# Modulation of the second layer: three sixths row chunk by row chunk on TensorE in the first MLP, the last sixth in the second MLP

## The chip, the cores and the metric

The kernel runs on one core of one Trainium2 chip. The metric is the device time of one execution, in microseconds (us). One execution was also profiled; its trace gives the start and the length of every instruction on the engines: TensorE (PE, its weight loads are PEld), VectorE (DVE), ScalarE (ACT), GpSimd (POOL) and SyncE, whose queue SP issues nearly all transfers.

## What is computed

Two layers over 512 latent tokens (`x`) and 256 context tokens (`c`), 1024 wide, in float32. Each layer modulates its normalised tokens by shift, scale and gate vectors that come from a conditioning vector, one for each of the two token kinds; this modulation is what the change touches:

```python
for l in range(DEPTH):
    last = l == DEPTH - 1
    mod_x = (jax.nn.silu(c) @ w_ada[l] + b_ada[l])[:, None, :]
    sh1, sc1, g1, sh2, sc2, g2 = jnp.split(mod_x, 6, axis=-1)
    mod_c = jax.nn.silu(c_ctx) @ w_ada[l] + b_ada[l]
    csh1, csc1, cg1, csh2, csc2, cg2 = jnp.split(mod_c, 6, axis=-1)
    ...
    hx = rmsnorm(x, g_pre_mix[l]) * (1.0 + sc1) + sh1
    ...
    x = x + g1 * rmsnorm(y, g_post_mix[l])
    hx2 = rmsnorm(x, g_pre_ff[l]) * (1.0 + sc2) + sh2
    x = x + g2 * rmsnorm(squared_relu_mlp(hx2, w_ff1[l], w_ff2[l]), g_post_ff[l])
```

`w_ada[l]` is 1024 x 6144, so each sixth (shift, scale, gate for the mixing, then the same for the MLP) is a product of a vector with a 1024 x 1024 matrix. In the last layer only shift and scale of the mixing (`csh1`, `csc1`) are still needed for the context tokens. The MLP is `square(relu(h @ w1)) @ w2` with 4096 hidden features.

## The kernel before

**Precision.** Large products run in float32r: each operand is split into a high and a low part, and a product takes three matmuls (high by high, high by low, low by high). Splitting a weight costs a cast on ScalarE (`hi`, or the first half of a tile `Wf`) and a subtraction on VectorE or GpSimd (`lo`, the second half). All raw weights, those of the modulation too, go through the same four buffers (tag "raw", 512 KB each); a load is issued by SP, in program order of its queue, as soon as the buffer it takes has been released.

**The MLP of a layer** runs in 16 hidden groups of 256 features (groups 0 to 15). Groups 0 and 1 are plain (`ff1`, tiles `h...`). For groups 2 to 15 the first product of the latent tokens is done in Winograd's form: `wino_open` builds seven weight operands from two raw tiles (casts L1147, low parts L1148, differences L1152), `wino` multiplies them (L1182, tiles `w` and `wt`; those with `t` take sums `S` of token blocks, made by `wino_a`, L952 to L956) and multiplies the context tokens plainly (L1195, `wc`); `hidden` squares the result (L1122 to L1125), and L1201 adds partial sums. The second product (`ff2`, tiles `f2`, layer, group, token kind, L1247) then goes token block by token block, six blocks in layer 0 and four in layer 1, and VectorE adds its PSUM result to `Y` (L1251).

**The modulation** is a generator, `ada_quad`, one per sixth `(l, q)`. It loads `w_ada` in eight row chunks of 128 rows (tile `wa`, L252) and has two ways to use them:

- With `side` (an accumulator in SBUF): VectorE multiplies a chunk by its 128 entries and adds it up, `acc` (L264 the first, L266 the others), one instruction per chunk and token kind, each followed by a `yield`. After the last chunk TensorE sums over the 128 partitions with a stationary operand that has a column of ones (L272): four matmuls per token kind, each 32 columns of the array wide.
- Without `side`: TensorE multiplies each chunk (L279), four matmuls per chunk, both token kinds at once (they are two of the 32 columns of `silu`); they accumulate in one PSUM tile over the eight chunks. One `yield` per chunk.

Both end in the same way: the row is copied to SBUF (`arow`) and turned into columns, or, for a gate (q = 2 or 5), multiplied by its gain and written to DRAM.

After each block of `ff2` from group 1 on, the MLP loop takes one step of the generator (`next(ada, None)`), and behind the last group it takes what is left. In layer 0 that is the gate of its own MLP, `(0, 5)`, and all six sixths of layer 1; all seven go with `side`: `(0, 5)`, `(1, 0)` and `(1, 1)` for two token kinds (16 steps each), the other four for one (8 each), 80 in all. Earlier sixths of layer 0 go without `side` beside the attention.

The program's order is not the engines' order: a scheduler reorders instructions within each engine by priority and by when it thinks that their operands are there; each engine then runs its list in order.

Of the kernel before, what the change touches and what calls it, by code (L numbers as in the profile page):

```python
# [3 lines left out]

# [14 lines left out]
P = 128  # L19
# [12 lines left out]
# How far the first product of the MLP goes ahead of other work.  # L32
HP = 5
# The engine (v or p) that takes each of the two-operand steps of a hidden group: low parts of the weights of the
# first and second product, differences of weights, low parts of the hidden features.
# [10 lines left out]
# What the tensor engine does beside the attention units of a layer: U, G, F load the weights of a column group  # L46
# of the in-projection and u, g, f project a token block with them, fc, fx step through the Fourier mixing,
# gc, gx load the gates, oc, ox step through the output projection, ada through a modulation.
# [13 lines left out]
def _bc(ap, n, axis):  # L62
    """ap with a broadcast dimension of n put in at free position `axis`."""
    v = ap.unsqueeze(axis)
    shape = list(v.shape)
    shape[axis] = n
    return v.to_broadcast(shape)
# [3 lines left out]
def kernel(ctx: ExitStack, tc: tile.TileContext, a: dict, out: bass.AP):  # L71
# [15 lines left out]
    # Temporaries of a chain come from h1, h2, h3 in this order, so that chains never wait in a circle.  # L87
# [9 lines left out]
    # Streams that run side by side have tiles of their own; within a tag tiles are handed out in program order.  # L97
# [25 lines left out]
    F = bank("F", 3)  # L123
# [9 lines left out]
    # ------------------------------------------------------------- constants  # L133
# [18 lines left out]
    def rows_in(name, width, pairs):  # L152
        """Rows at given partitions of a zeroed [32, width] tile."""
        t = act.tile([32, width], F32, name=name, tag="slot")
        nc.gpsimd.memset(t, 0.0)
        for r0, src in pairs:
            nc.sync.dma_start(t[r0:r0 + src.shape[0], :], src)
        return t

    def turned(t, name, use):  # L160
        """Feature-major pieces of four chunks of such rows in PSUM, handed to `use`."""
# [7 lines left out]
    # silu(c), silu(c_ctx) as two columns of a zero-padded stationary operand  # L169
# [37 lines left out]
    # ---------------------------------------------------- common small helpers  # L207
# [4 lines left out]
    def power(o, i, scale, bias, expo):  # L212
        """o = (i * scale + bias) ** expo"""
# [11 lines left out]
    def wunit(src, shape, name, lo_eng=None, part=None, hi_pool=False):  # L225
        """A weight unit in two float32r parts whose sum is the float32 weight."""
# [11 lines left out]
    # ------------------------------------------------------------------ adaLN  # L238
    # modc[l]: feature-major columns for (sh1, sc1, sh2, sc2); gates go to DRAM rows.
# [7 lines left out]
    def ada_quad(l, q, alloc, alloct, wtile, side=None):  # L247
        """A sixth of the modulation of a layer. side: the rows of the weight times their entries are summed over
        the row chunks beside the tensor engine, which is left with the sum over the partitions."""
# [73 lines left out]
    def ada_rest(steps, alloc, alloct, side=None):  # L323
        """Steps through (layer, quad), one row chunk of the weight at a time."""
# [8 lines left out]
    # ------------------------------------------------- feature-major activations  # L333
    class Feat:
        """Feature-major tokens in two float32r parts, eight chunks of 128 features: with a tile for
        every chunk (whole=True, wide moving operands) or tiles for every token block."""
# [20 lines left out]
        def dests(self, k2, b0):  # L357
            """Destinations (hi, lo, slice of the [128, 2, 256] source) for chunks 2 k2, 2 k2 + 1."""
# [23 lines left out]
    def modulate(xns, feat, b0, l, which, alloc, order=range(KD // 2)):  # L382
        """Normalised token blocks b0, b0 + 1 -> modulated, feature-major, in two parts."""
# [14 lines left out]
    # ------------------------------------------------------------- projections  # L398
# [14 lines left out]
    def in_group(l, nm, c0, c1, feats, consume, alloc, alloc2, units=None):  # L413
        """Loads a column group of w_in; the function returned projects one token block. What `consume` puts
        into `later` comes behind the products of the next block."""
# [19 lines left out]
    def rotate(ps, rope, nh, which, b, name):  # L435
        """Rotary embedding of a token-major [128, nh * 64] block in PSUM."""
# [14 lines left out]
    # ------------------------------------------------------------------ layers  # L451
    feats0 = {"c": Feat("c", "f00", False), "x": Feat("x", "f00", False)}
    # The start: shift and scale come a quarter of the features at a time, and behind each quarter the products
    # of its features with columns 256 .. 768 of the in-projection for the token blocks that are there.
# [8 lines left out]
    def ada_quarter(f):  # L463
        """Columns f * 256 .. of shift and scale of layer 0; four row chunks at a time share the tensor engine."""
# [46 lines left out]
    def layer(l, feats):  # L511
# [15 lines left out]
        # ---- in-projection and what follows from each column group  # L527
# [43 lines left out]
        def got_q(j, kind, b, ps, alloc):  # L571
            """Heads 4 j .. 4 j + 3: rotated, scaled, high parts over low parts along the partitions."""
# [24 lines left out]
        def gelu2(ps, out_, name):  # L597
            """out_ = 2 gelu(ps), in the tanh form; returns the [128, 256] temporary it used."""
# [60 lines left out]
        def part1(kind, k, hl, t0, n):  # L659
            """Tokens t0 .. t0 + n of a chunk of the gating and Fourier features."""  # L660
# [4 lines left out]
        def finish_s(kind, msf, nb):  # L665
            """msf: [128, nb], the mean squares of the Fourier part (plus eps) of every block."""
# [19 lines left out]
        def fourier(kind):  # L686
            """Three steps, for other work to lie between them."""
# [726 lines left out]
```

## Time and profile before

| | us |
|---|---|
| runs of the kernel, lowest, median, highest of three | 1513.12, 1518.51, 1522.53 |
| span of the profiled execution | 1516.8 |
| TensorE busy (matmuls) | 1429.4 |
| VectorE busy | 1115.8 |
| ScalarE busy | 747.7 |
| GpSimd busy | 644.3 |

Both MLPs lie between the mixing stages: that of layer 0 from about 350 to 950 us, that of layer 1 from about 1150 us to the end. In the table of stretches a row gives, for each engine, the busy time and the number of instructions, then the granted TensorE clock (1.00 is 2.4 GHz, 0.50 is 1.2 GHz), the mean busy share of the 16 DMA engines and what they moved in GB/s. In a timeline a row is a run of like instructions: start, time to the end of the last, engine, line, operation, output and inputs, shapes, count, and in brackets the idle time ahead of it. Matmuls are pipelined, so the time at which the next row starts tells what a row held of TensorE; its own length does not.

### The profile page before, as it was taken

The page shows a single profiled execution, that of the slowest core. Times are in us where ns is not written, and L with a number is a line of the kernel's source. Part 1 is how long each engine was busy: PE and PEld are TensorE (multiplying, and loading weights), DVE is VectorE, ACT ScalarE, POOL GpSimd, SP SyncE. Part 2 cuts the span into 40 slices and gives each one's busy share as a digit, 9 for nine tenths or more (in the row PEclk, how much of TensorE's full clock was granted, in tenths as well). Part 3 has the DMA queues.
Part 4 walks back from the last instruction along what each step waited for, and adds up shares of the span by engine and source line. Part 5 has one row for each costly group of instructions (what it writes and reads, how often), then busy time and mean ns, then how long its engine had stood idle before and what let it go on. Part 6 is the DMA issues. An engine that isn't in the chain of part 4 may idle for free. (4 is left out here: it accounts for less than half of the span.)

```text
span 1516.8 us, 24509 instructions
## 1 busy us (share of the span) xinstructions
PE 1429.4 (94%) x9133; PEld 1252.7 (83%) x9133; DVE 1115.8 (74%) x2003; ACT 747.7 (49%) x1673; POOL 644.3 (42%) x608
## 2 busy tenths in 40 slices
PE   7999999999899999999989998999998899999997
PEld 4688798788788878888878887998777788989886
DVE  3366887858687877878777758788757987777685
ACT  3346666556534333343333445476656555554452
POOL 3212636646634333334433546234346644344241
PEclk9999999999999999999999999999998999999999
DMA  9634322435132332325554344213134133223322
GB/s 328 228 122 154 112 74 84 137 115 167 42 100 84 124 111 84 126 70 174 167 172 129 125 160 139 72 55 87 39 100 165 56 112 111 93 89 100 110 84 84
DMA packets 94352, 177.58 MB, mean 117 GB/s; under 512 B 5796, under 2 KB 59524, under 8 KB 94232
## 3 DMA queue, kind: packets, MB, share of 16 engines
q1 hardware_dynamic: 91224, 170.93, 35.0%
q0 software_dynamic: 3008, 5.08, 1.2%
q8 instruction: 72, 1.18, 0.3%
q14 instruction: 48, 0.39, 0.1%
HBM read 166.62 MB, written 9.46 MB: 116 GB/s over the span
## 5 line engine op out<-in xcount | busy, mean ns | idle before, releaser
L1152 POOL TENSOR_TENSOR raw_f<-raw_f,raw_f 128x512 f32<-128x512 f32 x70 | 98.2, 1402 | 107.8 <-DVE raw_f L1152 89.5
L1147 ACT CAST Wf<-raw_f 128x512 fp32r<-128x512 f32 x98 | 60.4, 619 | 118.6 <-DMA raw_f<-in_w_ff 108.4
L266 DVE SCALAR_TENSOR_TENSOR acc<-wa,silu,acc 128x1024 f32<-128x1024 f32 x70 | 96.1, 1391 | 21.7 <-DMA wa<-in_w_ada 21.6
L1148 POOL TENSOR_TENSOR Wf<-raw_f,Wf 128x512 fp32r<-128x512 f32 x28 | 40.1, 1433 | 153.3 <-ACT Wf L1147 153.3
L1195 PE MATMUL wc<-f01c,Wf 128*128 128x256 f32 x672 | 98.5, 286 | 3.4 <-DVE p L1201 3.4
L1195 PEld LDWEIGHTS wc<-f01c,Wf 128*128 128x128 f32 x672 | 91.6, 194 | 7.9 <-DVE p L1201 3.8
L1148 DVE TENSOR_TENSOR Wf<-raw_f,Wf 128x512 fp32r<-128x512 f32 x70 | 62.0, 887 | 41.0 <-ACT Wf L1147 40.9
L234 ACT CAST hi_f<-raw_f 128x1024 fp32r<-128x1024 f32 x72 | 73.8, 1043 | 34.8 <-PE f208c L1247 6.6
L235 POOL TENSOR_TENSOR lo_f<-raw_f,hi_f 128x1024 fp32r<-128x1024 f32 x20 | 54.7, 2735 | 77.7 <-ACT hi_f L234 57.6
L1125 DVE TENSOR_TENSOR hx<-r,hx 128x256 fp32r<-128x256 f32 x98 | 61.5, 630 | 31.2 <-ACT r L1124 31.1
L235 DVE TENSOR_TENSOR lo_f<-raw_f,hi_f 128x1024 fp32r<-128x1024 f32 x52 | 76.6, 1478 | 1.3 <-ACT hi_f L234 1.0
L1123 ACT ACTIVATE hx<-r 128x256 fp32r<-128x256 f32 x112 | 45.4, 413 | 44.4 <-PE f203x L1247 8.7
L1182 PE MATMUL w<-f11x,Wf 128*128 128x256 f32 x336 | 65.1, 283 | 0.0
L1182 PE MATMUL w<-S,Wf 128*128 128x256 f32 x336 | 63.0, 283 | 0.0
L1122 ACT ACTIVATE r<-c 128x256 f32<-128x256 f32 x84 | 34.7, 414 | 55.5 <-DVE c L1201 43.4
L1182 PEld LDWEIGHTS w<-f11x,Wf 128*128 128x128 f32 x336 | 54.7, 191 | 1.5
L1182 PEld LDWEIGHTS w<-S,Wf 128*128 128x128 f32 x336 | 53.0, 191 | 1.7 <-issue 0.4
L1182 PE MATMUL w<-f01x,Wf 128*128 128x256 f32 x336 | 50.4, 284 | 1.9 <-ACT Wf L1147 1.0
L1182 PEld LDWEIGHTS w<-f01x,Wf 128*128 128x128 f32 x336 | 46.4, 191 | 5.3 <-ACT Wf L1147 1.4
L1124 ACT ACTIVATE r<-r 128x256 f32<-128x256 f32 x112 | 45.5, 413 | 1.9
L393 ACT ACTIVATE xvx<-xTx,mod 128x256 f32<-128x256 f32 x64 | 31.6, 560 | 18.2 <-PE xTx L379 11.9
L797 ACT ACTIVATE E0x<-E0x,mx_0x 128x512 f32<-128x512 f32 (+1 forms) x32 | 24.9, 778 | 12.9 <-DVE mx_0x L791 12.7
(1243 smaller groups left out, 4886.1 us busy)
## 6 DMA issues: line engine op xcount, KB each, us to landing
raw_f<-in_w_ff SPq DMA_DIRECT2D x128, 512.0 KB
wa<-in_w_ada SPq DMA_DIRECT2D x80, 512.0 KB
wq<-in_w_ada SPq DMA_DIRECT2D x16, 512.0 KB
raw_out0c<-in_w_out SPq DMA_DIRECT2D x8, 512.0 KB
raw_out0x<-in_w_out SPq DMA_DIRECT2D x8, 512.0 KB
res0x<-xr0x SPq DMA_DIRECT2D x8, 512.0 KB
raw_out1x<-in_w_out SPq DMA_DIRECT2D x8, 512.0 KB
xl0x<-in_x SPq DMA_DIRECT2D x4, 512.0 KB
```

The source lines that it names most:

```text
L234: nc.scalar.copy(hi, raw)
L235: (lo_eng or nc.vector).tensor_tensor(out=lo, in0=raw, in1=hi.bitcast(F32), op=ALU.subtract)
L266: nc.vector.scalar_tensor_tensor(out=acc[r], in0=w, scalar=s, in1=acc[r], op0=ALU.mult, op1=ALU.add)
L1122: nc.scalar.activation(r, src, AF.Relu)
L1123: nc.scalar.activation(hv[:, 0], r, AF.Square)
L1124: nc.scalar.activation(r, r, AF.Square)
L1125: next(lo_h).tensor_tensor(out=hv[:, 1], in0=r, in1=hv[:, 0].bitcast(F32), op=ALU.subtract)
L1147: nc.scalar.copy(t[:, 0], src)
L1148: next(lo).tensor_tensor(out=t[:, 1], in0=src, in1=t[:, 0].bitcast(F32), op=ALU.subtract)
L1152: next(diff).tensor_tensor(out=o, in0=x, in1=y, op=ALU.subtract)
L1182: nc.tensor.matmul(ps, W[w][:, wl, k], A[k // 2][:, k % 2, xh], start=(m == 0), stop=(m == 11))
L1195: nc.tensor.matmul(ps, W[f"{k // 4 + 1}{j + 1}"][:, wl, k % 4], f2["c"].ap(k, xh, 0, CTX), start=(m == 0), stop=(m == 3 * KD - 1))
```

## The change

`(0, 5)`, `(1, 0)` and `(1, 1)` lose their `side`: in the first MLP they go row chunk by row chunk through TensorE, with their sum in bank V of PSUM and the turned row in T. `(1, 2)`, `(1, 3)` and `(1, 4)` stay as they were. `(1, 5)` moves into the MLP of layer 1. The generator of the first MLP has 48 steps in place of 80, that of the second has 8 in place of none; one step is still taken behind each block of `ff2`. Comments are gone too, and line numbers are one higher from the top on because of the import.

```diff
+from itertools import chain
...
         if not last:
             ada_start(l + 1)
-            ada = ada_rest([(l, 5)] + [(l + 1, q) for q in range(6)], T, V, xl)
+            ada = chain(ada_rest([(l, 5), (l + 1, 0), (l + 1, 1)], V, T), ada_rest([(l + 1, q) for q in (2, 3, 4)], T, V, xl))
+        else:
+            ada = ada_rest([(l, 5)], T, V, xl)
```

**First piece of order**, TensorE, where the Winograd products of hidden group 4 in layer 0 begin (`Wf104t` is a weight operand of that group, `S` the sums of token blocks, `wc` the context product, `wa` a chunk of `(1, 1)`). Before:

```order
L1195 MATMUL wc_5611<-f01c_3212,Wf_5551 128x256 x2
L1182 MATMUL wt_5641<-S_4652,Wf104t_5555 128x256 x6
L1182 MATMUL wt_5641<-S_4671,Wf104t_5555 128x256 x6
L1182 MATMUL wt_5654<-S_4657,Wf104t_5559 128x256 x6
L1182 MATMUL wt_5654<-S_4676,Wf104t_5559 128x256
```

Now:

```order
L1196 MATMUL wc_5680<-f01c_3212,Wf_5620 128x256 x6
L1183 MATMUL wt_5710<-S_4652,Wf104t_5624 128x256 x6
L280 MATMUL ada_5581<-wa_5901,silu 32x256
L1183 MATMUL wt_5710<-S_4671,Wf104t_5624 128x256
L280 MATMUL ada_5581<-wa_5901,silu 32x256
L1183 MATMUL wt_5710<-S_4671,Wf104t_5624 128x256
L280 MATMUL ada_5581<-wa_5901,silu 32x256
L1183 MATMUL wt_5710<-S_4671,Wf104t_5624 128x256
L280 MATMUL ada_5581<-wa_5901,silu 32x256
L1183 MATMUL wt_5710<-S_4671,Wf104t_5624 128x256 x3
```

The four matmuls of one chunk stand between those of a Winograd product, each by itself. Elsewhere the four of a chunk stand together, or four and part of the next chunk's.

**Second piece of order**, SP, where groups 1 and 2 of the first MLP are loaded (L228 or L229 are second-product weights and what `out_proj` and `ff1` load, L1133 or L1134 the weights of a Winograd group, here group 2). Before:

```order
L228 DMA raw_f_4704<-in_w_ff 128x1024
L252 DMA wa_4728<-in_w_ada 128x1024
L252 DMA wa_4764<-in_w_ada 128x1024
L887 DMA res0x_4090<-xr0x_4077 128x1024
L252 DMA wa_4800<-in_w_ada 128x1024
L1133 DMA raw_f_4820<-in_w_ff 128x4x256
L1133 DMA raw_f_4822<-in_w_ff 128x4x256
```

Now:

```order
L229 DMA raw_f_4704<-in_w_ff 128x1024
L253 DMA wa_4727<-in_w_ada 128x1024
L253 DMA wa_4749<-in_w_ada 128x1024
L888 DMA res0x_4090<-xr0x_4077 128x1024
L253 DMA wa_4771<-in_w_ada 128x1024
L253 DMA wa_4793<-in_w_ada 128x1024
L253 DMA wa_4815<-in_w_ada 128x1024
L253 DMA wa_4837<-in_w_ada 128x1024
L1134 DMA raw_f_4843<-in_w_ff 128x4x256
L1134 DMA raw_f_4845<-in_w_ff 128x4x256
```

Six chunks instead of three stand ahead of the weights of group 2; the same holds for the groups that follow, up to group 8. Before, groups 9 to 13 had six.

**Third piece of order**, SP, where groups 1 and 2 of the second MLP are loaded. Before:

```order
L228 DMA raw_f_13009<-in_w_ff 128x1024
L887 DMA res1x_12506<-xr1x_12493 128x1024
L228 DMA raw_f_13015<-in_w_ff 128x1024
L1133 DMA raw_f_13085<-in_w_ff 128x4x256
L1133 DMA raw_f_13087<-in_w_ff 128x4x256
```

Now:

```order
L229 DMA raw_f_12970<-in_w_ff 128x1024
L888 DMA res1x_12467<-xr1x_12454 128x1024
L229 DMA raw_f_12976<-in_w_ff 128x1024
L253 DMA wa_12999<-in_w_ada 128x1024
L253 DMA wa_13018<-in_w_ada 128x1024
L888 DMA res1x_12519<-xr1x_12506 128x1024
L253 DMA wa_13037<-in_w_ada 128x1024
L253 DMA wa_13056<-in_w_ada 128x1024
L149 DMA xr1x_16239<-res1x_12323 128x1024
L1134 DMA raw_f_13059<-in_w_ff 128x4x256
L1134 DMA raw_f_13061<-in_w_ff 128x4x256
```

Four chunks of `(1, 5)` stand ahead of the weights of group 2 there; the other four stand ahead of those of group 3.

## Rows read from the trace of the kernel before

**Rows 1.** The page, its first part: busy time, share of the span and instructions of TensorE, its weight loads and the other engines.

```profile
PE 1429.4 (94%) x9133; PEld 1252.7 (83%) x9133; DVE 1115.8 (74%) x2003; ACT 747.7 (49%) x1673; POOL 644.3 (42%) x608
```

**Rows 2.** The table by stretches over the first MLP: its Winograd groups' start, their run, and the passage to layer 1.

```profile
402.00:450.00 48.00, 39.83 (x230) 35.01 (x229) 43.87 (x52) 18.06 (x34) 24.63 (x16) 0.93 0.26 79
450.00:836.50 386.50, 368.17 (x2306) 325.08 (x2305) 299.89 (x408) 145.75 (x318) 149.56 (x102) 1.00 0.40 127
836.50:960.00 123.50, 115.42 (x743) 102.13 (x743) 88.00 (x147) 62.20 (x146) 64.82 (x64) 1.00 0.39 128
```

**Rows 3.** What TensorE waited for from 400 to 455 us: who waited, for whom, us in total, times, longest.

```profile
PE f201c L1247 <- DVE lo_f L235: 3.0, 1, 3.0
PE wt L1182 <- DVE p L1201: 2.0, 1, 2.0
PE f201c L1247 <- ACT hi_f L234: 1.6, 1, 1.6
PE wt L1182 <- DVE S L953: 1.6, 2, 1.0
```

**Rows 4.** Groups of instructions from 340 to 870 us: VectorE's multiply-adds and first products of the chunks; behind the count busy us, mean ns of one, idle us ahead of them and what ended it.

```profile
L266 DVE SCALAR_TENSOR_TENSOR acc<-wa,silu,acc 128x1024 f32<-128x1024 f32 x70 | 96.1, 1391 | 21.7 <-DMA wa<-in_w_ada 21.6
L264 DVE TENSOR_SCALAR acc<-wa,silu 128x1024 f32<-128x1024 f32 x10 | 8.2, 819 | 3.9 <-DMA wa<-in_w_ada 2.4 <-PE ada L272 1.4
```

**Rows 5.** The instructions of line 279, chunks on TensorE beside the attention of layer 0: shortest, median and longest in ns, first and last start in us, shape.

```profile
L279 PE MATMUL ada<-wa,silu x192: 379/379/404, 49.5 to 164.9; 128*32 128x256 f32 x192
```

**Rows 6.** Timeline of TensorE in the first MLP, around closing sums of sixths (L272).

```profile
468.07 0.39 PE L1247 MATMUL f202x<-lo_f,hx 128*128 128x512 f32 x1
468.30 0.39 PE L1247 MATMUL f202x<-hi_f,hx 128*128 128x512 f32 x1
468.62 0.63 PE L272 MATMUL ada<-acc,unit 128*32 128x256 f32 x6
469.18 0.50 PE L1247 MATMUL f202x<-hi_f,hx 128*128 128x512 f32 x1
469.52 0.39 PE L1247 MATMUL f202x<-lo_f,hx 128*128 128x512 f32 x1
...
470.77 1.05 PE L272 MATMUL ada<-acc,unit 128*32 128x256 f32 x10
471.75 0.38 PE L1182 MATMUL w<-S,Wf 128*128 128x256 f32 x1
...
888.22 0.64 PE L272 MATMUL ada<-acc,unit 128*32 128x256 f32 x8
888.78 0.97 PE L1247 MATMUL f2014x<-hi_f,hx 128*128 128x512 f32 x3
```

**Rows 7.** Timeline of TensorE beside the attention, around chunk matmuls (L279) that stand in small numbers.

```profile
160.19 0.62 PE L279 MATMUL ada<-wa,silu 128*32 128x256 f32 x4
160.74 0.51 PE L825 MATMUL pv0c<-PT0c,Vc 128*128 128x512 f32 x1
161.18 0.62 PE L279 MATMUL ada<-wa,silu 128*32 128x256 f32 x2
161.73 0.33 PE L634 MATMUL pm0c<-vs0c,wsT 128*128 128x128 f32 x1
```

**Rows 8.** The table by stretches in slices of 10 us (columns as in rows 2).

```profile
410.00:420.00 10.00, 6.07 (x25) 4.64 (x24) 10.00 (x7) 1.75 (x4) 8.70 (x5) 0.83 0.43 132
420.00:430.00 10.00, 7.39 (x39) 6.64 (x40) 10.00 (x12) 1.67 (x3) 1.66 (x2) 0.85 0.22 70
```

**Rows 9.** The same for line 266 alone: its busy time on VectorE, then clock, DMA share and GB/s.

```profile
402.00:450.00 48.00, 7.40 (x6) 0.93 0.26 79
```

**Rows 10.** The table by stretches, cut where `(1, 1)` ends and the sixths for one token kind begin (columns as in rows 2).

```profile
455.00:687.90 232.90, 224.41 (x1405) 198.48 (x1406) 180.22 (x246) 89.15 (x197) 88.50 (x61) 1.00 0.32 102
687.90:836.50 148.60, 138.82 (x862) 121.86 (x860) 115.52 (x160) 54.17 (x115) 58.07 (x40) 0.99 0.51 161
```

**Rows 11.** What TensorE waited for in the whole program (columns as in rows 3).

```profile
PE wt L1182 <- DVE S L953: 5.4, 4, 2.9
...
PE ada L279 <- DMA wa<-in_w_ada: 0.7, 1, 0.7
```

**Rows 12.** Timeline of SP's queue at the start of the second MLP: the weights of the first Winograd group.

```profile
1149.98 2.53 SPq L1133 DMA_DIRECT2D raw_f<-in_w_ff  x2
```

**Rows 13.** Timeline of VectorE there: the first low parts of these weights.

```profile
1172.17 1.29 DVE L1148 TENSOR_TENSOR Wf<-raw_f,Wf 128x512 fp32r<-128x512 f32 x2
```

**Rows 14.** The table by stretches at the start of the second MLP (columns as in rows 2).

```profile
1150.00:1160.00 10.00, 8.98 (x61) 8.73 (x62) 7.89 (x11) 4.77 (x12) 5.81 (x8) 0.83 0.89 307
1160.00:1170.00 10.00, 10.00 (x70) 9.20 (x70) 3.67 (x6) 6.02 (x14) 4.32 (x5) 1.00 0.17 57
...
1200.00:1210.00 10.00, 10.00 (x64) 9.31 (x64) 10.00 (x15) 3.75 (x8) 3.78 (x3) 0.91 0.35 107
1210.00:1220.00 10.00, 10.00 (x59) 8.76 (x58) 9.64 (x18) 7.44 (x17) 8.13 (x6) 1.00 0.17 52
```

## The prediction

> **What bounds the kernel now.** I read the page first: TensorE is busy for 1429.4 of 1516.8 us, VectorE for 1115.8 [rows 1]. The change works in the two MLPs, so I cut the first one out in a table by stretches [rows 2]. The reader is to see two stages in it. From 402 to 450 us VectorE is busy 43.87 of 48.00 us and TensorE only 39.83: VectorE is the limit. The list of what TensorE waited for there [rows 3] names VectorE for three of four waits (low parts of the second product's weights 3.0 us, partial sums 2.0, S sums 1.6) and a ScalarE cast (1.6). From 450 to 836.5 us TensorE is busy 368.17 of 386.50 us: TensorE is the limit, a microsecond put on it is paid nearly in full, and one taken from VectorE brings something only in a pause of TensorE. The idle that 402 to 836.5 us can give back is 8.2 + 18.3 = 26.5 us. That is the ceiling of what a lighter VectorE earns there, apart from the clock.
>
> **What VectorE loses.** Three sixths, two token kinds, eight row chunks: 6 first products and 42 multiply-adds. At 0.82 and 1.39 us [rows 4] that is 4.9 + 58.4 = 63 us off the first MLP. The last sixth, one product and seven multiply-adds, moves into the second: 0.82 + 9.7 = 10.6 us.
>
> **What TensorE gains in work.** 24 row chunks of four matmuls, each 32 columns of the array wide and 256 long. The attention stage runs the same form [rows 5]; the trace records each such matmul as two instructions. Its price depends on how many stand side by side. Four (x8) take from 888.22 to the next work at 888.78, 0.56 us; three (x6) 468.62 to 469.18, also 0.56; five (x10) 470.77 to 471.75, 0.98 [rows 6]. And a single one (x2) takes 161.18 to 161.73, 0.55 us: as much as four [rows 7]. There is a toll at both ends: a 512-column matmul of the MLP holds 0.23 us (468.07 to 468.30), but 0.32 ahead of such a piece (468.30 to 468.62) and 0.34 behind it (469.18 to 469.52) [rows 6]. So a piece of one to four costs 0.56 + 0.09 + 0.11 = 0.76 us, one of five to eight 0.98 + 0.20 = 1.18.
> The order of the changed kernel tells how the 96 matmuls stand: in 38 pieces, 34 of one to four (21 of these of a single matmul, as in the first piece of order in the part on the change) and four of six to eight. That is 34 × 0.76 + 4 × 1.18 = 30.6 us. The 24 closing matmuls that go stood in pieces of 3, 5, 8 and 8: 0.76 + 3 × 1.18 = 4.3 us. **Net +26.3 us on TensorE.** The pieces that come lie in hidden groups 1 to 4; 18 of them, 13.7 us, in one stretch from the last products of group 3 into those of group 4.
>
> **What the lighter VectorE gives back.** *402 to 450 us:* the 8.2 us of idle, and the clock, which the two slices from 410 to 430 us show at 0.83 and 0.85 with 13.5 us of busy TensorE [rows 8]; at full clock these would take some 2 us less. Bounds 0 and 10.2. VectorE loses 7.4 us here [rows 9], but these steps stand behind 422 us while the pauses begin at 404. On the other hand the weights of the next group now come behind six chunk loads instead of three (second piece of order), so that their splitting leaves VectorE to the S sums and low parts that are waited for. I take 6.
> *450 to 836.5 us:* up to 687.9 us, where a sixth of two kinds runs with three chunk loads per group, TensorE idles 232.90 - 224.41 = 8.5 us in seven groups, 1.2 each; behind that, with one kind and six loads per group, 148.60 - 138.82 = 9.8 us in four, 2.4 each [rows 10]. Both have six VectorE steps per group, so the loads make the difference. Now groups 1 to 8 have six loads each and the last five none: four groups go from 1.2 to 2.4 (+5), the last ones lose theirs (-9.8), and the lowered clock in them (0.99 over 148.6 us) about 1.5. I take -6; bounds -13 and +5.
>
> **What may wait anew.** A chunk lies in one of four buffers that the weights of the MLP use too. VectorE freed them; now TensorE does, at the chunk's place in its order. SP issues its loads in order, so the weights of the next hidden group queue behind the release of a chunk, and where a chunk is late it is TensorE that stands, with the products of the MLP behind it. VectorE's multiply-adds have waited 21.6 us for such loads [rows 4]; TensorE, in the attention stage, 0.7 us for 24 chunks [rows 11]. Bounds 0.7 and 22. The order leaves several products between a chunk's turn and the one before, so I stay nearer the small end: 4.
>
> **The second MLP.** Eight chunk loads, the 10.6 us on VectorE, and one closing piece that left the first MLP. Four of the loads stand ahead of the weights of the first Winograd group (third piece of order). Those weights were asked for at 1149.98 and used on VectorE at 1172.17 [rows 12, 13], 22 us later, and VectorE is busy only 3.67 of 10 us from 1160 to 1170 [rows 14]: four steps of 1.4 us fit in there, and this gap is the cover; without it they cost 5.5. The other four fall between 1200 and 1220, where VectorE is busy 10.00 and 9.64 of 10 [rows 14] and still makes the S sums, for which TensorE waits 5.4 us in the whole program [rows 11], 1.6 of it in the first MLP [rows 3] and so 3.8 here. Bounds 0 and 10.6; I take 3.
>
> **Sum:** 26.3 - 6 - 6 + 4 + 3 = +21 us. The profiled execution would go from 1516.8 to 1538; the median of the runs is 1.7 us above it (1518.5), which makes **1539.5** on their scale.
>
> **Rivals.**
> *VectorE was the limit throughout.* All pauses from 402 to 836.5 us go, 26.5 us and 3.5 us of clock, and no new wait comes: 1518.5 + 26.3 - 30 + 3 = 1518, no change. For it: the waits of [rows 3] are mostly VectorE's. Against: from 450 us on TensorE pauses only 18.3 us in 386, and VectorE's load stays as it is in groups 5 to 8.
> *A quarter of the price.* If tiles of 32 columns overlapped with whatever is beside them, a matmul would cost 0.14 us (0.56 / 4 [rows 6]) wherever it stands: (96 - 24) × 0.14 = +10. With the 30 us of pauses gone this gives 1518.5 + 10 - 30 = 1498.5, faster. It decides once more than 25 of the 30 us come back. Against it: the single one at 0.55 us [rows 7].
> The Trainium skill (TensorEngine Tiling, Overview and Key Properties) gives this rival its rule: 32 columns let four tiles run at once, up to four times as fast, and tiles work independently; it adds that a change of tiling mode drains the engine. The trace agrees with the first only inside a piece.
> *The buffers bind.* TensorE waits for chunks, or for the weights behind them, as long as VectorE did, 22 us instead of 4: 1518.5 + 21 + 18 = 1557.5. For it: 2.4 us of idle per group with six loads. Against: the transfers have room, 161 GB/s there [rows 10] against 307 at another place [rows 14].
>
> **Chances.** The forecast (+12 to +30 us) 0.60, VectorE as the limit 0.18, a quarter of the price 0.06, the buffers 0.16. The range leaves out 1 in 10 on either side: below it the quarter price and a little of the full relief, above it the worse half of the buffers' case. That is 1518 to 1556. About 1% (15 us) is what a measurement of this kernel tells from no change. Slower by more than that: 0.50 of the forecast's 0.60 and all of the buffers' 0.16, 0.66. Within it: the rest of the forecast, the relief and a third of the quarter price, 0.30. Faster: 0.04.
>
> **What would show it.** Right: pieces of chunk matmuls in the first MLP at 0.55 us with a toll at both ends, single ones too; TensorE's busy time up by about 26 us and its idle between 402 and 836 us down by some 10; the groups with TensorE's chunks longer by 4 us and more, the last five shorter by about 2 each. Wrong: single ones near 0.14 us; TensorE's waits for chunks over 10 us; a second MLP longer by more than 10; the stretch from 402 to 450 us with as much idle as before.

## The result, and the profile after

| | before | after |
|---|---|---|
| four runs each, median (lowest to highest), us | 1517.99 (1513.12 to 1522.53) | 1535.63 (1531.26 to 1539.39) |
| span of the profiled execution, us | 1516.8 | 1531.2 |
| TensorE busy, us | 1429.4 | 1452.6 |
| VectorE busy, us | 1115.8 | 1061.6 |

The changed kernel takes 1.0118 times as long, 95% interval 1.0097 to 1.0139: slower by 1.2%, 18 us on the medians and 14.4 us between the two profiled executions. The forecast was 1539.5 us, the range 1518 to 1556. The total is near, in part by luck: of the terms behind it two came out within 1 us, and two were off in opposite directions, by some 8 and 4 us. Of the experiments below one execution, of e7 at 4821 us, is in no median and no ratio.

The page's first part, to be read beside [rows 1]: VectorE lost 54 us, TensorE gained 23, and the gain decides.

```profile
PE 1452.6 (95%) x9277; PEld 1258.8 (82%) x9277; DVE 1061.6 (69%) x1955; ACT 750.3 (49%) x1673; POOL 634.0 (41%) x608
```

The table by stretches of the changed kernel, columns as in [rows 2]: the two stretches of there, then the same work as in [rows 10], cut at the first product `f2` of groups 2, 9 and 13.

```profile
402.00:450.00 48.00, 43.11 (x272) 31.56 (x271) 35.84 (x43) 19.04 (x36) 25.43 (x17) 0.93 0.51 165
450.00:836.50 386.50, 376.71 (x2324) 324.77 (x2323) 250.56 (x365) 144.03 (x312) 140.93 (x105) 0.99 0.37 114
...
449.40:719.30 269.90, 260.11 (x1601) 219.52 (x1600) 177.23 (x255) 99.66 (x213) 97.14 (x74) 0.99 0.43 135
719.30:850.10 130.80, 130.80 (x831) 118.81 (x830) 82.03 (x124) 52.05 (x116) 49.91 (x36) 1.00 0.21 65
```

Three things are to be seen. From 402 to 450 us TensorE idles 4.9 us instead of 8.2, at the same clock, 0.93. Up to 719 us it idles 9.8 us (8.5 before) although VectorE is now busy for 66% of the time there (77% before). In the last groups, without chunk loads, it never idles: 130.80 of 130.80 us, where 9.8 were lost in [rows 10].

What TensorE waited for in the first MLP, columns as in [rows 3]: for the chunks only 3.3 us, in three places.

```profile
PE wc L1196 <- DVE p L1202: 3.6, 2, 2.8
PE ada L280 <- DMA wa<-in_w_ada: 3.3, 3, 1.9
PE f201c L1248 <- DVE lo_f L236: 1.8, 1, 1.8
```

The timeline of TensorE around chunk matmuls (L280), to be read as [rows 6]: three together, a single one, and four.

```profile
507.09 0.39 PE L1248 MATMUL f203c<-hi_f,hc 128*128 128x512 f32 x1
507.41 0.63 PE L280 MATMUL ada<-wa,silu 128*32 128x256 f32 x6
507.97 0.50 PE L1248 MATMUL f203c<-hi_f,hc 128*128 128x512 f32 x1
...
514.50 0.62 PE L280 MATMUL ada<-wa,silu 128*32 128x256 f32 x2
515.05 0.39 PE L1196 MATMUL wc<-f01c,Wf 128*128 128x256 f32 x1
515.36 0.62 PE L280 MATMUL ada<-wa,silu 128*32 128x256 f32 x2
...
525.09 0.64 PE L280 MATMUL ada<-wa,silu 128*32 128x256 f32 x8
525.65 0.98 PE L1183 MATMUL wt<-S,Wf104t 128*128 128x256 f32 x6
```

Three hold 507.41 to 507.97, 0.56 us; one holds 514.50 to 515.05, 0.55; four hold 525.09 to 525.65, 0.56. Of the 21 single ones of this MLP 20 take 0.55; the other, at 412 us, takes 0.99, at a lowered clock (0.57 granted from 411 to 414 us). The toll is there too: the one `wc` between two pieces holds 0.31 us (515.05 to 515.36), and three of that width between two pieces 0.55 (442.85 to 443.40 in the rows of e12 below), so 0.12 each and 0.19 of toll, 0.20 forecast.

**The account.** I cut the traces at the first product of group 0 of the first MLP (`f200x`) and at the first product of layer 1 (`pin1kvxx`), add up TensorE's idle time in between, and charge each piece of modulation matmuls 0.76 us (1.18 for five to eight).

| first MLP, us | before | after | difference |
|---|---|---|---|
| length | 540.9 | 550.1 | +9.2 |
| modulation matmuls | 7.3 | 32.8 | +25.5 |
| TensorE idle | 28.8 | 15.0 | -13.8 |
| the rest (clock, order) | 504.8 | 502.3 | -2.5 |

The row of the modulation matmuls is the forecast's price times the pieces, so it can't test the price. The trace can: from the start of each piece to the next work, less the waits, the pieces of this MLP hold TensorE for 6.0 us in all before (8 pieces) and 25.4 after (41). With 0.2 us of toll for each of the 33 more this is +26.

Everything behind it grew from 594.5 to 601.3 us (+6.8), and the part ahead shrank by 1.6: 9.2 + 6.8 - 1.6 = +14.4. The loss behind it lies in groups 1 and 2 of the second MLP, from the first `f211x` to the first `f213x`: this stretch takes 51.5 to 52.4 us in the five kernels below that move the sixth as the change does (the changed one among them) and 44.1 to 45.0 in the eight that have none of its chunks there. The table by stretches there, before:

```profile
1198.20:1242.30 44.10, 44.10 (x267) 39.57 (x266) 39.97 (x61) 21.48 (x45) 21.47 (x15) 0.96 0.30 96
```

and after: 8.2 us longer, 4.8 of it idle (2.5 ahead of the closing sum of the sixth, 1.3 for the sums `Y1x`, 1.0 for `hx`). The other 3.4 are busy time: the closing sum's piece (0.8), a lower clock (0.94 for 0.96) and a rest that is not told apart.

```profile
1205.70:1258.00 52.30, 47.51 (x274) 40.92 (x274) 45.68 (x65) 21.51 (x44) 24.82 (x16) 0.94 0.41 131
```

The queue of SP there, before:

```profile
1200.40 5.51 SPq L1133 DMA_DIRECT2D raw_f<-in_w_ff  x2
```

and after: the weights of group 3 are asked for some 20 us later, behind four chunks, 13 of it counted from `f211x` of the same kernel.

```profile
1207.85 10.58 SPq L253 DMA_DIRECT2D wa<-in_w_ada  x4
1221.16 2.84 SPq L1134 DMA_DIRECT2D raw_f<-in_w_ff  x2
```

The chain of work that ended last, followed back over 1200 to 1262 us of the changed kernel (start, length, what):

```profile
1222.39 1.21 DVE acc L267
1223.62 3.83 DMA raw_f<-in_w_ff
...
1229.40 3.48 POOL raw_f L1153
1232.88 1.25 POOL Wf113t L1149
...
1240.90 5.12 DMA raw_f<-in_w_ff
...
1246.05 0.63 ACT Wf L1148
...
1246.70 1.32 DVE Wf L1149
...
1249.00 0.64 PE ada L273 x8
...
1250.38 5.61 PE w L1183 x36
```

This is how a buffer shows in a profile. VectorE's last multiply-add on a chunk ends at 1223.6, and in that moment a load of weights starts: the chunk's buffer was what it waited for. GpSimd and VectorE make the weight operands from the weights, the closing sum comes behind, then the products. In the kernel before the same view names TensorE nearly all along:

```profile
by line: PE wt L1182 30.1%; PE f211x L1247 23.6%; PE f212x L1247 22.4%; PE w L1182 17.2%; DVE S L953 3.4%; PE f213x L1247 2.8%; DVE s L956 1.4%; issue 0.1%
```

### The profile page after: what moved, and what is told of

It reads as the page before. It is cut to its first block, busy times and chain, and to the rows that moved or that the text cites. A ratio compares the mean times of both kernels' runs of the same rounds, so it can differ in the third digit from the quotient of the medians.

```text
span 1531.2 us, 24740 instructions
## 1 busy us (share of the span) xinstructions
PE 1452.6 (95%) x9277; PEld 1258.8 (82%) x9277; DVE 1061.6 (69%) x1955; ACT 750.3 (49%) x1673; POOL 634.0 (41%) x608
## 5 line engine op out<-in xcount | busy, mean ns | idle before, releaser
L1149 DVE TENSOR_TENSOR Wf<-raw_f,Wf 128x512 fp32r<-128x512 f32 x70 | 70.0, 1001 | 49.6 <-ACT Wf L1148 49.4
L267 DVE SCALAR_TENSOR_TENSOR acc<-wa,silu,acc 128x1024 f32<-128x1024 f32 x28 | 37.8, 1350 | 18.0 <-DMA wa<-in_w_ada 18.0
L280 PE MATMUL ada<-wa,silu 128*32 128x256 f32 x384 | 45.1, 394 | 3.8 <-DMA wa<-in_w_ada 3.8
L394 ACT ACTIVATE xvx<-xTx,mod 128x256 f32<-128x256 f32 x64 | 31.8, 560 | 16.5 <-PE xTx L380 13.3
```

Source lines behind the costliest of these rows:

```text
L1149: next(lo).tensor_tensor(out=t[:, 1], in0=src, in1=t[:, 0].bitcast(F32), op=ALU.subtract)
```

## The experiments

Lengths are those of the profiled execution: "first" from `f200x` to `pin1kvxx`, "behind" from there to the end. Each ratio is to runs of the kernel before that were taken together with that kernel (medians 1516.19 to 1517.99). The last column varies by itself: the six kernels whose last sixth stays in the first MLP lie between 589.7 and 596.5 (mean 592.9), the five that move it as the change does between 600.5 and 604.6 (mean 601.8). So the move costs 7 to 9 us there, and a difference of a few between two profiles says little.

| kernel | median, us | ratio to before | first, us | behind, us |
|---|---|---|---|---|
| before | | | 540.9 | 594.5 |
| after | 1535.63 | 1.0118 [1.0097, 1.0139] | 550.1 | 601.3 |
| e1_pieces_of_four | 1584.48 | 1.0433 [1.0410, 1.0457] | 603.6 | 600.5 |
| e2_last_sixth_stays | 1531.04 | 1.0084 [1.0066, 1.0102] | 558.0 | 594.5 |
| e3_last_sixth_moves_alone | 1517.73 | 1.0007 [0.9993, 1.0022] | 535.1 | 601.1 |
| e4_steps_start_a_group_later | 1524.60 | 1.0034 [1.0016, 1.0052] | 547.5 | 596.5 |
| e5_pieces_by_priority | 1531.36 | 1.0090 [1.0062, 1.0117] | 542.8 | 601.7 |
| e6_last_loads_left_out | 1509.42 | 0.9949 [0.9931, 0.9967] | 533.2 | 589.7 |
| e7_last_steps_cut | 1519.42 | 1.0019 [1.0005, 1.0034] | 543.5 | 590.6 |
| e8_second_mlp_without_loads | 1529.78 | 1.0085 [1.0068, 1.0102] | 547.8 | 601.4 |
| e9_loads_spread_evenly | 1527.02 | 1.0067 [1.0050, 1.0085] | 550.9 | 591.2 |
| e10_last_sixth_moves_thinly | 1533.36 | 1.0110 [1.0092, 1.0127] | 540.1 | 611.3 |
| e11_both_spread | 1533.11 | 1.0111 [1.0094, 1.0129] | 542.7 | 606.7 |
| e12_one_matmul_of_four | 1525.64 | 1.0059 [1.0039, 1.0079] | 537.9 | 604.6 |

### What does a piece of chunk matmuls cost?

**e1_pieces_of_four**, the changed kernel with the four matmuls of a chunk made indivisible:

```diff
-                for g in range(4):
...
+                with tc.tile_critical() if l or q == 5 else ExitStack():
+                    for g in range(4):
+                        nc.tensor.matmul(ps[32 * g:32 * g + 32, :], silu[:, k, :], w[:, g, :],
...
```

> The changed kernel with the four matmuls of a chunk kept together in TensorE's order in the MLP: 24 pieces of four in place of 38 pieces, same matmuls, same loads. Price by pieces (a lone matmul costs as much as four, 0.76 us with its tolls): 30.6 - 24 x 0.76 = 12.4 us less than the changed kernel, 1523 us (1519 to 1527). Quarter price (0.14 us per matmul wherever it stands): no difference, 1535.6. Buffers (the loss is in loads and late chunks): at most a few us less, 1532 to 1537.

Measured 1584.5: a miss, and no answer on the price. The fence also holds the piece at its place against all other work. What TensorE waited for from 380 to 960 us:

```profile
PE ada L281 <- DMA wa<-in_w_ada: 11.7, 4, 3.8
PE ada L281 <- DMA raw_f<-in_w_ff: 10.4, 3, 3.6
PE ada L281 <- issue: 6.2, 6, 4.0
```

TensorE stands ahead of the pieces, for their chunks and for weights that they need not have waited for. It does show what the rival of the binding buffers would have looked like: TensorE standing 11.7 us for chunks.

**e5_pieces_by_priority**, the same with a priority instead of a fence (`tc.high_priority(offset=0)` in the place of `tc.tile_critical()`):

> The changed kernel with the four matmuls of a chunk drawn together by a priority scope in the scheduler instead of an indivisible section: 25 pieces for 96 matmuls, 20.3 us by my prices in place of 30.6; loads and VectorE's steps in nearly the same order. Price by pieces: 1535.6 - 10.3 = 1525 (1521 to 1529). Quarter price: 1534 to 1537. Buffers: 1532 to 1537.

The total, 1531.4, misses the 1521 to 1529 expected from the price by pieces, and lies just below what the buffers' rival gave. By price the pieces fall from 32.8 to 22.5 us in its trace. The first MLP fell by 7.3 us, TensorE's idle rose by 2.0. By the totals (1.0090 against 1.0118) the gain is some 4 us, with intervals that overlap: in the right direction, not proven by the total.

**e12_one_matmul_of_four** is e5 without three quarters of the columns in row chunks 1 to 7 of the three sixths, 63 of 96 matmuls:

```diff
...
-                for g in range(4):
...
+                    for g in range(4 if k == 0 or (l, q) not in ((0, 5), (1, 0), (1, 1)) else 1):
...
```

> The changed kernel with the chunk's matmuls kept by priority as in the run of pieces by priority (1531.4), and of the four matmuls of a chunk only the first for row chunks 1 to 7 of the three sixths: it leaves out three quarters of their columns, 63 of 96 matmuls. 23 pieces remain where there were 25; 20 of them are single matmuls where 17 were fours. If a piece costs 0.76 us whether it holds one matmul or four, the first MLP saves 20.3 - 17.9 = 2.4 us: 1529 (1527 to 1531). If a matmul of 32 columns costs 0.14 us wherever it stands, 63 x 0.14 = 8.8 us go: 1522.5.

The total (1525.6) lies between the two expectations, its interval overlaps that of e5, and the profiled spans differ by 2.5 us (1524.4 and 1521.9). The first MLP is 4.9 us shorter than in e5, what lies behind 3.0 longer, so neither length tells 2.4 from 8.8. The rows decide. The timeline of TensorE in e5, pieces of four:

```profile
475.59 0.64 PE L281 MATMUL ada<-wa,silu 128*32 128x256 f32 x8
476.16 1.33 PE L1184 MATMUL wt<-S,Wf103t 128*128 128x256 f32 x9
477.42 0.64 PE L281 MATMUL ada<-wa,silu 128*32 128x256 f32 x8
477.99 2.30 PE L1184 MATMUL wt<-S,Wf103t 128*128 128x256 f32 x17
```

and in e12, where one of the four is left:

```profile
442.29 0.64 PE L281 MATMUL ada<-wa,silu 128*32 128x256 f32 x8
442.85 0.62 PE L1184 MATMUL wt<-f01x,Wf102t 128*128 128x256 f32 x3
443.40 0.62 PE L281 MATMUL ada<-wa,silu 128*32 128x256 f32 x2
443.95 0.62 PE L1184 MATMUL wt<-f01x,Wf102t 128*128 128x256 f32 x3
```

0.57 us for four, 0.55 for one. Taking three quarters of a piece away frees 0.02 us of TensorE. So it is over the whole first MLP: less their waits and without the tolls, the pieces hold TensorE for 18.0 us in e5 (28 pieces) and 15.5 in e12 (26), 2.4 less for 63 matmuls less, where 0.14 us each would be 8.8. The rival of the quarter price falls.

### What did moving the last sixth cost?

**e2_last_sixth_stays**, the changed kernel with `(1, 5)` back in the first MLP:

```diff
-            ada = chain(..., ada_rest([(l + 1, q) for q in (2, 3, 4)], T, V, xl))
-        else:
-            ada = ada_rest([(l, 5)], T, V, xl)
+            ada = chain(..., ada_rest([(l + 1, q) for q in (2, 3, 4, 5)], T, V, xl))
```

> The changed kernel with the last sixth back in the first MLP, behind the others, so that nothing of the modulation is in the second MLP. If the second MLP pays for its eight chunks what the two traces differ by there (14.4 us at the end less 7.5 us at the start of its group 1, 6.9 us), and groups 9 and 10 pay 1 to 2 us each for them, 1535.6 - 6.9 + 3 = 1532 (1528 to 1534). If the second MLP hides them: 1536 to 1539.

**e3_last_sixth_moves_alone**, the kernel before with nothing but that move:

```diff
-            ada = ada_rest([(l, 5)] + [(l + 1, q) for q in range(6)], T, V, xl)
+            ada = ada_rest([(l, 5)] + [(l + 1, q) for q in range(5)], T, V, xl)
+        else:
+            ada = ada_rest([(l, 5)], T, V, xl)
```

> The kernel before with only the last sixth moved into the second MLP. If the second MLP pays 6.9 us for it and the first gets 2 to 4 us back: 1518 + 4 = 1522 (1520 to 1525). If the second MLP hides it: 1514 to 1516.

The lengths of the two agree. Where the sixth stays, the first MLP is 7.9 us longer and what lies behind 6.8 shorter than in the changed kernel; where it moves alone, the first is 5.8 shorter and the rest 6.7 longer. e2's total lies where it was expected if the second MLP pays; e3's, 1517.7, lies between its two expectations, because the first MLP got back more than the 2 to 4 us put there. By e3's total the move is a wash; by e2's it costs 5 us (1.0084 against 1.0118, the intervals just overlap). Either way most of the 18 us, 13 or more, is what the chunks on TensorE cost, net of what the lighter VectorE gave back. The stretch from `f211x` to `f213x` in e3 looks as in the changed kernel:

```profile
1194.50:1246.40 51.90, 47.08 (x275) 40.53 (x275) 48.28 (x64) 21.13 (x43) 24.13 (x16) 0.95 0.41 132
```

**e8_second_mlp_without_loads**, the changed kernel whose `(1, 5)` multiplies a matrix that already lies in SBUF; it leaves out eight loads, VectorE's steps remain:

```diff
-                w = load(k)
+                w = _bc(ident, 8, 1) if (l, q) == (DEPTH - 1, 5) else load(k)
...
```

> The changed kernel without the eight chunk loads of the last sixth in the second MLP; VectorE does its steps there on a constant matrix (that gate is not the reference's). The interval from the second product of group 2 to that of group 3 is 30.9 us in the changed kernel and 19.9 in the one before. If the loads push the weights of group 3 back: 20 to 22 us and 1528 to 1530 in all. If VectorE's steps do it: 29 to 31 and 1534 to 1537.

The pause between groups 2 and 3 went (`f212x` to `f213x` 21.0 us instead of 30.9) and the total, 1529.8, is the one that was put on the loads. But the part behind the first MLP is as long as with the loads, 601.4 us; the profiled execution is shorter in the first MLP, which is the same. And the steps did not stay where they were: with nothing to wait for they all moved to 1161 to 1176 us, ahead of group 1. The stretch from `f211x` to `f213x`:

```profile
1203.00:1251.90 48.90, 46.31 (x274) 40.26 (x273) 45.27 (x64) 25.12 (x51) 26.43 (x19) 0.93 0.30 97
```

That is 3.4 us less than with the loads, and still 4.8 more than in the kernel before, with no chunk load and no step in it: VectorE has 45.3 us of other work there instead of 40.0, presumably what the steps ahead put off. So the late weights are less than half of the 8.2 us, as far as this run separates them, and VectorE's time is presumably the rest. Up to `f211x` nothing changed (275.6 us from `pin1kvxx`, 275.8 with the loads); behind `f213x` this run is 3.7 us longer (276.9 against 273.2), but without chunks there the other kernels vary between 269.7 and 276.0 as well, so no cause is named.

**e10_last_sixth_moves_thinly**, the kernel before with that sixth moved, one chunk per group from group 4 on; the 72 steps that stay in the first MLP are spread over its 78 places as well:

```diff
...
+                if g is not None and g >= 4:
+                    next(ada, None)
...
-                    next(ada, None)
+                    step(72, g if b == 1 and kd == "x" else None)
```

> The kernel before with the last sixth moved into the second MLP, but one row chunk per hidden group from group 4 on in place of eight at groups 1 and 2. Moved in one lump it cost the second MLP 6 us and saved the first 5.8. Theory (the second MLP loses because four loads stand ahead of the weights of group 2 and four ahead of group 3, and VectorE is full there): spread out they cost the second MLP 0 to 2 us and the whole goes to 1513 (1511 to 1516). Rival (a load and its VectorE step cost the second MLP the same wherever they stand): 1518.

Both theories fall: the part behind the first MLP took 611.3 us, 17 more than before and 10 more than with the eight chunks in two lumps of four. (The first took 540.1, 5 more than in e3: presumably the spread steps took back what the move had saved.) VectorE's row for the multiply-adds there (columns as in [rows 4]) tells why:

```profile
L266 DVE SCALAR_TENSOR_TENSOR acc<-wa,silu,acc 128x1024 f32<-128x1024 f32 x7 | 9.0, 1284 | 13.3 <-DMA wa<-in_w_ada 13.3
```

9.0 us of work, 13.3 us of standing. One of the seven, on SP's queue:

```profile
1267.32 0.33 SPq L252 DMA_DIRECT2D wa<-in_w_ada  x1
```

on VectorE:

```profile
1268.69 0.41 DVE L1201 TENSOR_TENSOR c<-p,w 128x256 f32<-128x256 f32 x1
1271.32 1.28 DVE L266 SCALAR_TENSOR_TENSOR acc<-wa,silu,acc 128x1024 f32<-128x1024 f32 x1 [2.23 <-DMA wa<-in_w_ada]
1272.52 0.75 DVE L1125 TENSOR_TENSOR hx<-r,hx 128x256 fp32r<-128x256 f32 x2
...
1274.57 1.28 DVE L1251 TENSOR_TENSOR Y1x<-Y1x,f214x 128x512 f32<-128x512 f32 x2
```

and on TensorE:

```profile
1275.30 0.50 PE L1247 MATMUL f214x<-hi_f,hx 128*128 128x512 f32 x1 [1.23 <-DVE Y1x L1251]
```

The chunk is asked for at 1267.3, VectorE comes to its step at 1269.1 and stands for 2.2 us; the sums `Y1x` stand behind the step in its order, and TensorE waits 1.2 us for one of them. Over the whole second MLP TensorE waits 12.0 us for `Y1x`, 3.9 in the kernel before: 8 of the 17 us. The Trainium skill (PSUM — Partial Sum Buffer, Engine vs sequencer instructions) states that VectorE's queue is strictly first in, first out; this row agrees.

### What slows the last groups of the first MLP?

**e6_last_loads_left_out**, the kernel before without the chunk loads of the last four sixths; VectorE multiplies a matrix that lies in SBUF:

```diff
-                w = load(k)
+                w = load(k) if l == 0 or q < 2 else _bc(ident, 8, 1)
...
```

> The kernel before, without the chunk loads of the last four sixths (32 loads; their modulation vectors are not the reference's): VectorE does its steps on a constant matrix that lies in SBUF. It asks what the last five groups of the first MLP gained in the changed kernel (148.5 us before, 130.8 after). If the chunk loads slowed them: 131 to 135 us there and 1500 to 1506 in all. If VectorE's steps did: 146 to 149 us and 1515 to 1519.

**e7_last_steps_cut** keeps the loads and leaves out 15 of 16 columns of these sixths' multiply-adds:

```diff
+                        cut = 256 if l == 0 or q < 2 else 16
-                        nc.vector.scalar_tensor_tensor(out=acc[r], in0=w, scalar=s, in1=acc[r],
+                        nc.vector.scalar_tensor_tensor(out=acc[r][:, :, 0:cut], in0=w[:, :, 0:cut], scalar=s,
...
```

> The kernel before, with all chunk loads, but VectorE's multiply-adds of the last four sixths cut to a sixteenth of their columns (the modulation vectors are not the reference's): some 28 steps of 1.3 us become short ones. If the loads slowed the last five groups: 146 to 149 us there, 1515 to 1519 in all. If VectorE's steps did: 131 to 135 and 1500 to 1506.

The loads weigh more, though e6 met neither expectation: its 138.7 us and 1509.4 in all lie between the two. The table by stretches from `f209x` to `f2013x` in e6:

```profile
690.00:828.70 138.70, 134.63 (x842) 118.13 (x841) 119.53 (x160) 53.85 (x118) 62.82 (x41) 1.00 0.20 65
```

and in e7:

```profile
690.00:841.20 151.20, 138.93 (x844) 121.72 (x843) 89.02 (x160) 55.73 (x117) 55.08 (x42) 0.97 0.50 159
```

With VectorE at 119.53 us of work but no loads, TensorE idles 4.1 us; with VectorE at 89.02 us and the loads, 12.3 (before: 9.8). Leaving the loads out gives 9.9 of the 17.8 us by which the changed kernel is shorter here; of the other 7.9, 4.1 are this idle and 3.0 the four closing pieces, which the changed kernel has elsewhere. Cutting the steps alone gives nothing. The list of VectorE's waits in that stretch says how the loads act. Before:

```profile
DVE acc L266 <- DMA wa<-in_w_ada: 10.6, 15, 1.5
```

and in e7:

```profile
DVE acc L267 <- DMA wa<-in_w_ada: 30.8, 21, 2.7
```

The steps that became short only wait longer: when a step ends is set by when its chunk lands, not by its work. This looks like the mechanism of e10 again: all of TensorE's waits in this stretch of e7 are for sums of VectorE. That each of these sums stood behind a step that waited was not followed one by one.

**e9_loads_spread_evenly**, the kernel before with its loads thinned out, and **e11_both_spread**, with that and e10's move (48 in the place of 56):

```diff
                         nc.vector.scalar_tensor_tensor(out=acc[r], in0=w, scalar=s, in1=acc[r],
                                                        op0=ALU.mult, op1=ALU.add)
-                    yield
+                yield
...
+            elif calls[0] * total // 78 > (calls[0] - 1) * total // 78:
+                next(ada, None)
...
-                    next(ada, None)
+                    step(56, g if b == 1 and kd == "x" else None)
```

> The kernel before with its 56 chunk loads of the first MLP spread evenly: one step per row chunk (both token kinds' VectorE steps in it), 56 steps over the 78 places, so that four or five loads stand ahead of each group's weights instead of three ahead of groups 2 to 9 and six ahead of groups 10 to 13. Theory (loads that stand close together slow the last groups): leaving the last 32 loads out gave 1509.4; here they stay and only thin out, about half of that gain, 1513 (1511 to 1516), with groups 9 to 13 some 5 us shorter and groups 2 to 8 little longer. Rival (each load costs its share wherever it stands): 1518, what the last groups win the first ones lose.

> The kernel before with both: 48 chunk loads spread evenly over the first MLP, all on VectorE, and the last sixth in the second MLP one chunk per group from group 4 on. Theory: the two gains add, 1510 (1507 to 1514). Rival (a load costs its share wherever it stands): 1518.

My theory that loads cost because they stand close together falls: thinned out they made the first MLP 10 us longer. VectorE's multiply-adds stood longer for their chunks than in [rows 4], over the same 340 to 870 us:

```profile
L266 DVE SCALAR_TENSOR_TENSOR acc<-wa,silu,acc 128x1024 f32<-128x1024 f32 x70 | 92.2, 1330 | 27.0 <-DMA wa<-in_w_ada 26.8
```

That is 5 us more of standing for 10 us of time; TensorE's idle grew by 6.4 us (28.8 to 35.2), and two steps now stand behind one place. These are not told apart. All of the loss lies ahead of `f205x`. e11 has both losses in part.

### Was VectorE the limit from 402 to 450 us?

**e4_steps_start_a_group_later**, the kernel before without steps behind group 1:

```diff
                 ff2([1], kd, b)
-                next(ada, None)
```

> The kernel before with no modulation steps behind the blocks of group 1, so that VectorE has none in the stretch from 402 to 450 us; they come at the end of the MLP instead. If VectorE's steps cost TensorE 6 us there (my term of the sum): the second product of group 2 starts at 449 us instead of 455 and the time is 1513 to 1516. If the pauses there come from the S sums and weights alone: the same start, 1518 to 1521.

It doesn't answer. The second product of group 2 starts at 454.2 us, hardly earlier, but VectorE's steps of group 2 moved up into the stretch, 6.3 us of them in the place of 7.4 [rows 9], and the steps that now come later made the kernel slower.

## Why the prediction was right, point by point

**Net work on TensorE, +26.3 us: right.** By price and pieces it is +25.5 (the 0.8 that is missing is the closing piece that moved to the second MLP), by what the pieces hold in the trace +26, with the toll and with singles at the price of four. The trace and e12 bear out the step on which all hung. The Trainium skill (TensorEngine Tiling, Overview and Key Properties) states that four tiles of 32 columns work at once. The trace agrees inside a piece, where four take 0.56 us; beside work of other width the runs show nothing of it, one takes 0.55.

**What comes back in the first MLP, -12, and the new waits, +4: too small, and with a cause that was half right.** Pauses gave 13.8 us back and the rest (clock, order) 2.5, 16.3 together where the two terms put 8. By stretches, in TensorE's idle: from `f200x` to `f205x` 4.1 us came back where -4 (402 to 450 us, without the clock) and +4 for the chunks were put; groups 5 to 8, "four groups go from 1.2 to 2.4 (+5)", paid 2.1; the last groups gave 9.8, as forecast; the passage behind them, for which nothing was put, gave 2.0. The clock from 402 to 450 us stayed at 0.93, so the 2 us of that part didn't come. "The loads make the difference" was right for most of the idle in the last groups (e6, e7), but not because they stand close together, six to a group: VectorE stands at a step whose chunk has not landed, and sums that TensorE waits for stand behind it (seen in e10, inferred here). That fits e9, where thinning the loads out did not help. For the 3.3 us from 402 to 450 us the cause stays open, since e4 didn't take VectorE's steps out.

**New waits, 4 us:** 3.3 for the chunks in the list of waits. Right.

**The second MLP, +3: too small, +6.8 (7 to 9 over all kernels).** The first four chunks were hidden as forecast (`f210x` to `f211x` 38.6 us, 38.3 before). The step that was mis-sized is "The other four fall between 1200 and 1220 ... Bounds 0 and 10.6; I take 3". The 3.8 us of waits for S sums on which it leaned end at 1197 us in the kernel before, ahead of that stretch, and hardly changed (3.6). And it priced the chunks as VectorE time alone. But they also hold the buffers of the next weights, as the chain through chunk, buffer, weights and splitting shows: of the 8.2 us between `f211x` and `f213x` some 3.4 went with the loads in e8, and 4.8 stayed, presumably as VectorE's time. The first part is the mechanism of the rival of the binding buffers, in a place where I had not put it.

**The sum.** 25.5 - 16.3 + 6.8 - 1.6 ahead of the stage = 14.4 in the profiled execution, where the forecast had 21; what came back too much and what the second MLP cost too much cancel in part, and so far the nearness of the total is luck. The rival of VectorE as the limit went halfway: about half of the 30 us came back, not enough to pay for the pieces.

## What to carry to other kernels

A matmul of few columns between full-width ones costs here as much as four of them together: count the pieces in which such matmuls stand, not the matmuls, before moving work from an idle engine to the one that bounds the kernel. A step on an in-order engine costs what it waits for, and what stands behind it waits too; so ask when its operand lands before asking how long it runs. (Loading a chunk a whole group ahead of its step would be the test; no run here tried it.) And a load that borrows a buffer of a weight stream also costs what the weight behind it loses by coming later.

## What was not expected of the hardware

VectorE's multiply-adds, cut to a sixteenth of their columns, left the kernel as slow as before: their waits grew from 10.6 to 30.8 us in the same groups (e7). And one chunk per group, asked for 1.8 us ahead of its step in the rows of e10, cost what lies behind the first MLP more (17 us for eight, VectorE standing 13.3 us at seven of them) than two lumps of four (7 us, VectorE standing 1.6 us at one).
